# Forming the Strassen sums of w_out: 160 transfers of 256 KB through SBUF tiles, or 16 transfers of 2 MB inside DRAM

## The chip, the core and the metric

The kernel runs on one core of one Trainium2 chip. A core has a matrix engine (TensorE, PE in the profile, with its weight loads as PEld), a vector engine (VectorE, DVE), a scalar engine (ScalarE, ACT), GpSimd (POOL) and SyncE (SP), which here issues transfers only. Sixteen DMA engines move data between DRAM and the on-chip memory SBUF, and also from DRAM to DRAM. Transfers that SP issues appear in the profile as queue q1, those that POOL issues as queue q0. The metric is the device time of one execution in microseconds; lower is better.

## The reference, cut to what matters

The reference computes one layer of a streaming encoder on 512 rows (T) of 2048 features (D), in float32:

```python
h = rmsnorm(x, g_pre[i])
proj = h @ w_in[i]
qkv, z_a, b_raw, a_raw, glu_in, z_b, gate_logits = jnp.split(proj, _split_points(), axis=-1)
...                                   # gated delta rule on qkv -> y_a, conformer convolution on glu_in -> y_b
mixed = (gate_a * y_a + gate_b * y_b) @ w_out[i]
x = x + rmsnorm(mixed, g_post[i])
e = p[i] @ w_ple_proj[i]
x = x + rmsnorm(jax.nn.sigmoid(x @ w_ple_gate[i]) * e, g_ple[i])
```

The change touches the product with `w_out` (2048 x 2048) alone. The kernel computes it by Strassen's scheme on 2 x 2 blocks of the weight, which needs four sums of blocks: T1 = B11 + B12, T3 = B12 + B22, T2 = T1 + B22 and T4 = T2 + B21. (The signs are in the operands on the other side.) Each block, in each of two column halves `jp`, is four pieces of 512 KB: 2 MB.

## The kernel before, in words

Every large product is done on the PE with float32 split in two parts, high and low, so that a product of one weight tile and one activation tile is three matmuls of 128 x 128 by 128 x 512. A weight piece comes from DRAM into a raw tile (SP issues it), ACT casts the high part (line 127 or 408), DVE or POOL forms the low part by a subtraction (line 128 or 308), and the PE reads both.

The stages, with the times at which the trace of before shows their matmuls:

- 0 to 45 us, `load_x` (lines 226 to 266). SP issues, in this order, pieces of `w_ple_proj` and of `x`, one row block of x (two transfers of 512 KB) for each piece; then constants, the first piece of `w_in`, sixteen stores of 256 KB to `pe_dram` (line 257), and then the next three pieces of `w_in`. For each row block ACT squares x (line 245), DVE forms a mean, POOL takes it to the power -1/2 (`xrs`, line 250), and DVE scales x (line 252). Meanwhile the PE multiplies `p` by `w_ple_proj` (lines 216 to 218). Then it transposes x (line 261) and begins on the z_b part of `w_in` (lines 184, 186, 188).
- 45 to 95 us, the first five tiles of z_b, in the same loop `gemm_cm`.
- 95 to 551 us, `z_phase`: three weight groups (z, ga, gb), each with two column halves, by the same Strassen scheme (matmuls on lines 421 to 423). Here the weight sums are formed as they are used: raw pieces in tiles `raw` and `zraw`, sums on DVE in `zt`, and the last block added by an accumulating transfer from POOL (line 369, 48 of them). Up to eight finished weight pieces stand ready for the PE in the pools `ring` and `zw` (four each).
- 551 to 1480 us, q, k, v and the delta rule head by head, with further parts of `w_in`, in `gemm_cm`. Side jobs are spread among the matmuls by `tick()`: each job is a generator that is advanced once in so many matmuls.
- 1480 to 2086 us, convolution, the branch products (`yp`).
- 2088 to 2249 us, the product with `w_out` (`f`, lines 1385 to 1387), which loads the sums from the DRAM tensor `wo_sums`.
- 2249 to 2436 us, the per-layer embedding.

`presum` (line 1002) forms the sums of `w_out` ahead of time. It is spawned as a side job after the first pair of heads (line 1040). In before it does it piece by piece: it takes blocks into SBUF tiles `wsum` out of the pool `slots` (21 tiles shared by all), some by accumulating transfers, and gives sums to `wo_sums`.

The order in which each engine's instructions stand is not that of the Python text. A scheduler places the whole program's instructions on each engine when the program is built. It keeps the dependencies, gives tiles out as they come free, and puts an instruction on an engine when its own reckoning says that it can go. So an instruction whose inputs are ready and which needs no tile can stand far ahead of its place in the text. On the chip each engine then takes its instructions strictly in that order, POOL and its transfers too.

Of the kernel before, what the change touches and what calls it, by code (L numbers as in the profile page):

```python
# [9 lines left out]
F32 = mybir.dt.float32  # L10
F32R = mybir.dt.float32r
AF = mybir.ActivationFunctionType
ALU = mybir.AluOpType
AX = mybir.AxisListType.X

P = 128
T = 512
# [64 lines left out]
def _body(ctx, tc, A, out):  # L82
    nc = tc.nc
# [7 lines left out]
    slots = ctx.enter_context(tc.tile_pool(name="slots", bufs=21, side="right"))  # L91
# [47 lines left out]
    jobs = deque()  # L139
    active = []  # L140

    def spawn(gen, period, key=None):
        active.append([gen, period, period, key])
# [24 lines left out]
    def w_in_tile(t):  # L168
        return A["w_in"][t]

    def gemm_cm(src, rhs, evac):
        if src is not None:
            prep_src.extend([src[0], src[1]])

        def job():
            ps = gps.tile([P, T], F32, tag="g", name="g")
            for qt in range(4):
                hi, lo = next_piece()
                for kk in range(4):
                    k = qt * 4 + kk  # L180
                    rh, rl = rhs[k]
                    wh = hi[:, kk * P:(kk + 1) * P]
                    wl = lo[:, kk * P:(kk + 1) * P]
                    mm(ps, wh, rh, start=(k == 0), stop=False)  # L184
                    tick()
                    mm(ps, wh, rl, start=False, stop=False)  # L186
                    tick()
                    mm(ps, wl, rh, start=False, stop=(k == NK - 1))  # L188
                    tick()
            evac(ps)  # L190
        jobs.append(job)
# [99 lines left out]
    B11, B12, B22, B21 = range(4)  # L291
# [369 lines left out]
    def evac_k(h):  # L661
        def f(ps):
            y = conv4(ps, 16 + h)
            kc = hd.tile([P, T], F32, tag="kc", name="kc", bufs=2)
            nc.scalar.activation(kc, y, AF.Silu)
            kq = hd.tile([P, NTT, 4, 64], F32, tag="kq", name="kq", bufs=4)
            nc.gpsimd.tensor_copy(kq[:, :, 0::3, :], kc.rearrange("p (t x i) -> p t x i", x=2, i=64))
            hstate[h].update(kc=kc, kq=kq)
        return f

    def evac_q(h):
        def f(ps):
            y = conv4(ps, h)
            nc.scalar.activation(hstate[h]["kq"][:, :, 1:3, :], y.rearrange("p (t x i) -> p t x i", x=2, i=64), AF.Silu)
        return f

    def evac_v(h):
        def f(ps):
            y = conv4(ps, 32 + h)
            vc = hd.tile([P, T], F32, tag="vc", name="vc", bufs=2)  # L680
            nc.scalar.activation(vc, y, AF.Silu)
            hstate[h].update(vc=vc)
        return f
# [315 lines left out]
    WO = A["w_out"]  # L999
    T1, T2, T3, T4 = range(4)  # L1000
    sums = dram.tile([2, 4, 4, P, 1024], F32, name="wo_sums")
    def presum():
        for jp in range(2):
            for q in range(4):
                cs = [slice(n * T, n * T + T) for n in range(2)]
                a = [slots.tile([P, T], F32, tag="s", name="wsum") for n in range(2)]

                def take(t, blk, add):
                    for n in range(2):
                        nc.gpsimd.dma_start(t[n], WO[jp, blk, q][:, cs[n]], **(dict(accum_op=ALU.add) if add else {}))  # L1010
                        yield

                def give(t, m):
                    for n in range(2):
                        nc.gpsimd.dma_start(sums[jp, m, q][:, cs[n]], t[n])
                        yield
                yield from take(a, B11, False)
                b = [slots.tile([P, T], F32, tag="s", name="wsum") for n in range(2)]
                yield from take(b, B12, False)
                yield from take(a, B12, True)  # L1020
                yield from take(b, B22, True)
                yield from give(a, T1)
                yield from give(b, T3)
                yield from take(a, B22, True)
                yield 24
                yield from give(a, T2)
                yield from take(a, B21, True)
                yield 24
                yield from give(a, T4)

    rest = deque([lambda i=i: zb_tile(i) for i in range(FILL, NK)] + [f for i in range(2) for f in (lambda i=i: glu_b(i), lambda i=i: glu_a(i))])
    for g in range(NH // 2):
        pair = (2 * g, 2 * g + 1)
        for h in pair:
            gemm_cm(w_in_tile(16 + h), hT, evac_k(h))
            gemm_cm(w_in_tile(h), hT, evac_q(h))
            gemm_cm(w_in_tile(32 + h), hT, evac_v(h))
        jobs.append(lambda g=g: spawn(group(g), HP, "heads"))
        if g == 0:
            jobs.append(lambda: spawn(presum(), 13, "presum"))  # L1040
        for _ in range(2):
            if rest:
                rest.popleft()()
# [584 lines left out]
    for tt in range(NTT):  # L1628
# [9 lines left out]
        for j in range(4):  # L1638
            s = e_t4[tt][j]
# [67 lines left out]
```

## Time and profile before

| | |
|---|---|
| median of 3 runs | 2436.77 us (2436.03 to 2437.53) |
| the profiled execution | 2438.2 us, its span 2436.4 us |
| PE busy | 2409.8 us of the span (99%) |
| DVE, ACT, POOL busy | 1785.5, 1208.0, 491.8 us |
| moved by DMA | 380.21 MB, mean 156 GB/s; by SP's queue 319.32 MB, by POOL's 54.54 MB |
| `presum`'s transfers | 96 into `wsum` and 64 out of it, 256 KB each, issued from 552.6 to 1219.4 us |

In the rows of a timeline the first number is the start in microseconds from the span's start, the second how long the group took; in brackets stands how long the engine was idle before, and what ended that. A row of windows gives, for a stretch of time, its length, the busy time of PE, PEld, DVE, ACT and POOL (with the count of instructions), the granted clock of the PE, the mean busy share of the 16 DMA engines, and what they moved in GB/s. A row of waits gives who waited for whom: the total, how often, the longest.

### The profile page before, as it was taken

The numbers are of one execution on the slowest core, as the hardware profiler recorded it, in microseconds if no ns is written. First come the engines' busy times: TensorE is split into PE (matmuls) and PEld (weight loads), VectorE is DVE, ScalarE is ACT, GpSimd is POOL, SyncE is SP. The second block draws the span as 40 slices with busy tenths as digits, with TensorE's granted clock in tenths as the row PEclk, the third lists the DMA queues.
The fourth block names the chain that finished last, engine by engine and source line by source line (L and its number), as shares of the span: only waits on it lengthen the run. The fifth ranks groups of instructions, "written<-read, shape, count | busy, mean of one in ns | idle before, by whom it ended". The sixth has DMA issues, their size and how long they took to land.

```text
span 2436.4 us, 33721 instructions
## 1 busy us (share of the span) xinstructions
PE 2409.8 (99%) x11962; PEld 1983.6 (81%) x11962; DVE 1785.5 (73%) x3355; ACT 1208.0 (50%) x2357; POOL 491.8 (20%) x521
## 2 busy tenths in 40 slices
PE   8999999999999999999999999999999999999998
PEld 7888888887788888888888887888887788788886
DVE  7878888777677776767777668999998654667644
ACT  6555545555655555554556554454424433554532
POOL 0001110013213031232200002998840000000000
PEclk9999999999999999999999999999999999999999
DMA  7567776757546262556522222443534332664552
GB/s 264 168 194 208 195 207 206 212 155 210 175 122 182 94 181 92 169 166 184 173 92 92 77 87 74 151 135 110 168 125 164 126 124 97 234 218 168 194 175 77
DMA packets 145289, 380.21 MB, mean 156 GB/s; under 512 B 16352, under 2 KB 24800, under 8 KB 145120
## 3 DMA queue, kind: packets, MB, share of 16 engines
q1 hardware_dynamic: 119008, 319.32, 39.3%
q0 software_dynamic: 23808, 54.54, 10.3%
q10 hardware_dynamic: 2304, 4.20, 0.5%
q8 instruction: 94, 1.54, 0.3%
q14 instruction: 75, 0.61, 0.1%
HBM read 329.75 MB, written 48.23 MB: 155 GB/s over the span
## 4 chain that ended last, share of the span: by engine, by line
PE 94%; DVE 3%; ACT 1%; issue 1%; DMA 1%; POOL 0%; SPq 0%; DVEq 0%; POOLq 0%; ACTq 0%
PE g L186 14%; PE g L188 14%; PE g L184 14%; PE zp L422 6%; PE zp L421 6%; PE zp L423 6%; PE yp L1095 4%; PE yp L1097 4%; PE yp L1093 4%; PE f L1385 2%; PE f L1386 2%; PE f L1387 2%; PE f L1558 2%; PE f L1557 2%; PE f L1556 2%; PE psB L709 1%
## 5 line engine op out<-in xcount | busy, mean ns | idle before, releaser
L186 PE MATMUL g<-hl,w 128*128 128x512 f32 x1536 | 610.4, 397 | 0.0
L188 PE MATMUL g<-hh,w 128*128 128x512 f32 x1536 | 609.2, 397 | 0.0
L184 PE MATMUL g<-hh,w 128*128 128x512 f32 x1536 | 608.3, 396 | 0.1
L127 ACT CAST w<-raw 128x512 fp32r<-128x512 f32 x588 | 357.6, 618 | 454.7 <-PE g L188 176.7
L128 DVE TENSOR_TENSOR w<-raw,w 128x512 fp32r<-128x512 f32 x474 | 327.2, 697 | 180.3 <-ACT w L127 177.4
L188 PEld LDWEIGHTS g<-hh,w 128*128 128x128 f32 x1536 | 289.0, 188 | 56.3 <-DVE w L128 2.6
L186 PEld LDWEIGHTS g<-hl,w 128*128 128x128 f32 x1536 | 289.0, 188 | 55.7 <-issue 1.4
L184 PEld LDWEIGHTS g<-hh,w 128*128 128x128 f32 x1536 | 289.1, 188 | 54.2 <-ACT w L127 0.5
L955 DVE SCALAR_TENSOR_TENSOR uc<-up,vec,uc 128x497 f32<-128x497 f32 (+29 forms) x390 | 282.3, 734 | 13.2 <-ACT uc L934 1.9
L128 POOL TENSOR_TENSOR w<-raw,w 128x512 fp32r<-128x512 f32 x114 | 146.6, 1301 | 59.6 <-ACT w L127 57.8
L656 DVE SCALAR_TENSOR_TENSOR cv<-g,vec,cv 128x511 f32<-128x511 f32 x144 | 106.4, 739 | 27.6 <-ACT cv L654 26.9
L1093 PE MATMUL yp<-w,uh 128*128 128x512 f32 x256 | 100.1, 393 | 0.9 <-DVE gt L1104 0.9
L1095 PE MATMUL yp<-w,uh 128*128 128x512 f32 x256 | 100.3, 392 | 0.1
L1095 PE MATMUL yp<-w,oh 128*128 128x512 f32 x256 | 100.1, 391 | 0.0
L1097 PE MATMUL yp<-w,ul 128*128 128x512 f32 x256 | 100.1, 392 | 0.0
L1097 PE MATMUL yp<-w,ol 128*128 128x512 f32 x256 | 99.5, 391 | 0.0
L1093 PE MATMUL yp<-w,oh 128*128 128x512 f32 x256 | 99.1, 389 | 0.0
L842 DVE TENSOR_TENSOR prod<-UT,VT 128x2 f32<-128x2 f32 (+30 forms) x248 | 87.5, 353 | 6.5
L1010 POOL DMA_DIRECT2D wsum<-in_w_out x96 | 75.4, 840 | 67.7 <-DMA wsum<-in_w_out 35.5
L1329 POOL TENSOR_TENSOR rmsm<-totm,mhalf_c 128x2 f32<-128x2 f32 x2 | 2.4, 1202 | 377.3 <-DVE totm L1327 377.3
L977 POOL TENSOR_TENSOR uc<-uc,pr 128x511 f32<-128x511 f32 (+29 forms) x60 | 76.0, 1267 | 8.3 <-ACT pr L976 7.7
L1385 PE MATMUL f<-wsp,oph 128*128 128x512 f32 x192 | 75.6, 393 | 1.7 <-ACT wsp L1366 1.7
(386 smaller groups left out, 4943.4 us busy)
## 6 DMA issues: line engine op xcount, KB each, us to landing
raw<-in_w_in SPq DMA_DIRECT2D x194, 512.0 KB, 3.4
wsum<-in_w_out POOLq DMA_DIRECT2D x96, 256.0 KB, 5.2
raw<-in_w_ple_gate SPq DMA_DIRECT2D x40, 512.0 KB, 3.9
wo_sums<-wsum POOLq DMA_DIRECT2D x64, 256.0 KB, 4.1
raw<-in_w_br_a SPq DMA_DIRECT2D x32, 512.0 KB, 3.3
raw<-in_w_br_b SPq DMA_DIRECT2D x32, 512.0 KB, 3.3
raw<-in_w_ga SPq DMA_DIRECT2D x24, 512.0 KB, 4.4
raw<-in_w_gb SPq DMA_DIRECT2D x24, 512.0 KB, 4.7
```

Source lines behind the costliest of these rows:

```text
L127: nc.scalar.copy(hi, rq)
L128: low_part[0].tensor_tensor(lo, rq, hi.bitcast(F32), ALU.subtract)
L184: mm(ps, wh, rh, start=(k == 0), stop=False)
L186: mm(ps, wh, rl, start=False, stop=False)
L188: mm(ps, wl, rh, start=False, stop=(k == NK - 1))
L421: mm(ps[pr][t], lh, wh, start=q + n == 0, stop=False)
L422: mm(ps[pr][t], ll, wh, start=False, stop=False)
L423: mm(ps[pr][t], lh, wl, start=False, stop=q == 3 and n == 1)
L955: pin(nc.vector.scalar_tensor_tensor(y[:, s:], u[:, 0:T - s], vv(w0 + TAPS - 1 - s), y[:, s:], ALU.mult, ALU.add))
L1093: mm(ps[tt], lh[:, b], wh, start=k == 0, stop=False)
L1095: mm(ps[tt], lh[:, b], wl, start=False, stop=False)
L1097: mm(ps[tt], ll[:, b], wh, start=False, stop=k == NK - 1)
```

## The change

Instead of 512 KB pieces that go through SBUF, `presum` moves whole blocks of 2 MB from DRAM to DRAM, in eight transfers for each column half: T1 = B11 and T3 = B12 as plain copies of `w_out`'s blocks, B12 and B22 added to them by accumulating transfers, T2 as a plain copy of T1 out of `wo_sums` and B22 added, T4 as a plain copy of T2 and B21 added. The plain ones go out as 32 rows of 16384 numbers (64 KB), the accumulating ones as 256 rows of 2048 numbers (8 KB). No tile of `slots` is used. The job's period is 130 matmuls in place of 13. What is computed and what is read later is as before. The change makes the file five lines shorter, so that lines after it have numbers five lower.

```diff
     def presum():
         for jp in range(2):
-            for q in range(4):
-                cs = [slice(n * T, n * T + T) for n in range(2)]
-                a = [slots.tile([P, T], F32, tag="s", name="wsum") for n in range(2)]
-
-                def take(t, blk, add):
-                    for n in range(2):
-                        nc.gpsimd.dma_start(t[n], WO[jp, blk, q][:, cs[n]], **(dict(accum_op=ALU.add) if add else {}))
-                        yield
-
-                def give(t, m):
-                    for n in range(2):
-                        nc.gpsimd.dma_start(sums[jp, m, q][:, cs[n]], t[n])
-                        yield
-                yield from take(a, B11, False)
-                b = [slots.tile([P, T], F32, tag="s", name="wsum") for n in range(2)]
-                yield from take(b, B12, False)
-                yield from take(a, B12, True)
-                yield from take(b, B22, True)
-                yield from give(a, T1)
-                yield from give(b, T3)
-                yield from take(a, B22, True)
-                yield 24
-                yield from give(a, T2)
-                yield from take(a, B21, True)
-                yield 24
-                yield from give(a, T4)
+            def put(m, blk, add):
+                nc.gpsimd.dma_start(sums[jp, m], WO[jp, blk], **(dict(accum_op=ALU.add, max_dma_last_dim=8192) if add else {}))
+
+            def copy(m, n):
+                nc.gpsimd.dma_start(sums[jp, m], sums[jp, n])
+            put(T1, B11, False)
+            yield
+            put(T3, B12, False)
+            yield
+            put(T1, B12, True)
+            yield
+            put(T3, B22, True)
+            yield
+            copy(T2, T1)
+            yield
+            put(T2, B22, True)
+            yield
+            copy(T4, T2)
+            yield
+            put(T4, B21, True)
+            yield
...
         if g == 0:
-            jobs.append(lambda: spawn(presum(), 13, "presum"))
+            jobs.append(lambda: spawn(presum(), 130, "presum"))
```

Since the new transfers need no tile, the scheduler places them elsewhere than the old ones. The first place is the beginning of POOL's instructions. `xrs` is the power of the mean for one row block of x, `zt` an accumulating transfer of the z phase, `Tc` to `vz` are cleared just after the z phase. Before:

```order
L100 MEMSET half_c 128x8
L102 MEMSET mhalf_c 128x8
L250 ISA
L250 TENSOR_TENSOR xrs<-xms,mhalf_c 128x1 x4
L369 DMA zt<-in_w_z 128x512 x16
L369 DMA zt<-in_w_ga 128x512 x16
L369 DMA zt<-in_w_gb 128x512 x16
L529 MEMSET Tc 128x512
```

Now, as far as the last group of the z phase begins:

```order
L102 MEMSET mhalf_c 128x8
L1005 DMA wo_sums<-in_w_out 32x16384
L250 ISA
L250 TENSOR_TENSOR xrs<-xms,mhalf_c 128x1 x2
L1005 DMA wo_sums<-in_w_out 32x16384
L250 TENSOR_TENSOR xrs<-xms,mhalf_c 128x1 x2
L1005 DMA wo_sums<-in_w_out 256x2048
L369 DMA zt<-in_w_z 128x512 x8
L1005 DMA wo_sums<-in_w_out 256x2048
L369 DMA zt<-in_w_z 128x512 x8
L1008 DMA wo_sums<-wo_sums 32x16384
L369 DMA zt<-in_w_ga 128x512 x8
```

The copy of T1 now stands ahead of everything of x, that of T3 between the second and the third row block, and the first accumulating transfer (T1 += B12) right behind the fourth; the following ones stand one behind each eight `zt` transfers of the z phase.

The second place is POOL behind the z phase, where before the first of the 160 transfers stood:

```order
L536 MEMSET Xz_4994 128x128
L537 MEMSET vz_4998 128x128
L828 COPY VT<-cst 128x256
L1010 DMA wsum<-in_w_out 128x512 x6
L1015 DMA wo_sums<-wsum 128x512 x3
```

and now the second column half begins:

```order
L536 MEMSET Xz_4994 128x128
L537 MEMSET vz_4998 128x128
L1005 DMA wo_sums<-in_w_out 32x16384
L667 COPY kq<-kc 128x4x2x64
L628 TENSOR_TENSOR tg<-cst,gl 128x512 x2
```

So the first half (`jp` = 0) has moved ahead of and into the z phase, and the second half stands where the first began. SP's own transfers stand in the same order as before through load_x and the first tiles of z_b.

## The prediction

> **What bounds the kernel now.** I read the page's busy times first, then the chain, then the PE's waits.
>
> ```profile
> PE 2409.8 (99%) x11962; PEld 1983.6 (81%) x11962; DVE 1785.5 (73%) x3355; ACT 1208.0 (50%) x2357; POOL 491.8 (20%) x521
> PE 94%; DVE 3%; ACT 1%; issue 1%; DMA 1%; POOL 0%; SPq 0%; DVEq 0%; POOLq 0%; ACTq 0%
> PE e_ps L216 <- ACT w L127: 6.1, 1, 6.1
> ```
>
> The PE is busy for 2409.8 of 2436.4 us and makes 94% of the chain; its idle time is 26.6 us in all, of which 6.1 us are the wait for the very first weights. So almost nothing can be won by freeing POOL, SBUF tiles or DMA engines. What can be lost is large: anything that makes the PE wait adds to the end one for one. The question is whether the moved transfers make it wait.
>
> Next I looked at how full the DMA engines are, by stretches: the first 60 us, the z phase, and the two stretches over which the old presum ran (552.6 to 1219.4 us).
>
> ```profile
> 0.00:10.00 10.00, 3.89 (x9) 2.77 (x10) 1.99 (x3) 3.77 (x5) 0.35 (x6) 1.00 0.80 265
> 10.00:20.00 10.00, 7.81 (x33) 5.83 (x32) 6.08 (x13) 7.41 (x15) 1.11 (x2) 1.00 1.02 402
> 20.00:30.00 10.00, 10.00 (x46) 8.19 (x45) 7.54 (x16) 8.37 (x16) 1.10 (x2) 1.00 1.04 404
> 30.00:40.00 10.00, 10.00 (x71) 8.81 (x70) 9.46 (x15) 7.61 (x14) 0.00 (x0) 1.00 0.90 320
> 40.00:50.00 10.00, 10.00 (x51) 8.18 (x50) 10.00 (x18) 5.72 (x11) 0.00 (x0) 1.00 0.23 80
> 80.00:530.00 450.00, 450.00 (x1987) 372.62 (x1986) 363.16 (x585) 229.92 (x386) 42.87 (x48) 1.00 0.69 198
> 552.00:680.00 128.00, 126.41 (x593) 101.09 (x592) 90.25 (x198) 70.23 (x124) 41.46 (x53) 1.00 0.67 196
> 680.00:1230.00 550.00, 549.94 (x3259) 453.95 (x3259) 393.50 (x982) 302.73 (x712) 122.81 (x169) 1.00 0.52 150
> ```
>
> Three things are to be seen. From 10 to nearly 40 us all 16 DMA engines are full, at 402 GB/s: this is the one stage where a transfer more delays every transfer behind it. In the z phase they are 69% busy while the PE never idles (450.00 of 450). And where the old presum ran, the PE lost 1.6 us (128.00 less 126.41) and nothing after 680 us.
>
> **What is removed.** 160 transfers and their tiles between 552 and 1220 us. POOL waited for them, the PE did not. All that can come back is the 1.6 us of the row 552:680, and part of that belongs to other waits; I take -1, with bounds 0 and -1.6.
>
> **The price of a 2 MB transfer.** No row shows one from DRAM to DRAM; the nearest are these:
>
> ```profile
> q1 hardware_dynamic: 119008, 319.32, 39.3%
> q0 software_dynamic: 23808, 54.54, 10.3%
> zt<-in_w_z POOLq DMA_DIRECT2D x16, 256.0 KB, 5.7
> wsum<-in_w_out POOLq DMA_DIRECT2D x96, 256.0 KB, 5.2
> wo_sums<-wsum POOLq DMA_DIRECT2D x64, 256.0 KB, 4.1
> ```
>
> Queue q1 has plain transfers only: 39.3% of 2436.4 us over 319.32 MB is 3.0 us of all engines for a MB, 6.3 us for 2.1 MB; at the 402 GB/s of the full stretch it is 5.2 us. Queue q0 took 10.3%, 250.9 us, for 54.54 MB. Of these, 32 takes and 64 gives of 0.262 MB are plain (25.2 MB, 75.5 us at q1's price). The rest, 175 us, is 48 zt and 64 accumulating takes, 29.4 MB: 6.0 us a MB, 12.5 us for 2 MB, twice a plain one.
>
> A copy inside DRAM reads and writes DRAM. If both pass at once it costs what one side costs, 5.2 us; if one after the other, a load and a store, 10.4. I take the middle, 8. The accumulating one reads two operands and writes one: two passes are 10.4, three are 15.7, and the row of those into SBUF gives 12.5. I take 13, close to that row.
>
> The Trainium skill ("DMA: Bandwidth & Descriptors", section "Latency and other measured facts") gives copies between DRAM tensors at full rate as 207 to 214 GB/s for each direction. By it a 2 MB copy is an estimated 9.8 us, and the sum below would be 3.6 us higher. No run shows it yet.
>
> **The start.** The order puts T1's copy right behind a memset on POOL, the copy of T3 behind the second `xrs`, T1's accumulation behind the fourth. When these stood, and what SP has under way:
>
> ```profile
> 0.77 0.10 POOL L102 MEMSET mhalf_c<- 128x8 f32 x1
> 18.43 0.56 POOL L250 TENSOR_TENSOR xrs<-xms,mhalf_c 128x1 f32<-128x1 f32 x1 [5.60 <-DVE xms L248]
> 29.26 0.55 POOL L250 TENSOR_TENSOR xrs<-xms,mhalf_c 128x1 f32<-128x1 f32 x1 [4.94 <-DVE xms L248]
> 2.58 7.92 DMA x<-in_x
> 10.59 1.16 ACT xjunk L245 x2
> 12.30 0.50 PE L216 MATMUL e_ps<-w,ph 128*128 128x512 f32 x1 [1.18 <-ACT ph L203]
> 18.93 15.56 SPq L257 DMA_DIRECT2D pe_dram<-e_sb  x16
> 34.54 1.54 SPq L122 DMA_DIRECT2D raw<-in_w_in  x3
> DMA to landing us min/median/max: 5.4/6.7/7.3
> 42.70 1.77 ACT L127 CAST w<-raw 128x512 fp32r<-128x512 f32 x3
> 45.73 0.39 PE L184 MATMUL g<-hh,w 128*128 128x512 f32 x1
> ```
>
> (The landing row is that of line 122 in the stretch 34 to 36.2 us, the three transfers above it.)
>
> *T1 = B11* begins at about 1 us, as SP's first loads do. The chain of waits goes through the x load (2.58 to 10.50), ACT's squares behind it and the cast of `ph`, for which the PE waits until 12.30. There is no slack here, since ACT begins 0.1 us after the landing. So what the copy takes from the engines is added to that landing: +8 (5.2 to 10.4).
>
> *T3 = B12 and T1 += B12* then fall into the full stretch. They stand on another queue than SP's, but SP's queue is never empty here (sixteen stores, then w_in), so once they are done it is late by their whole time, however the two queues share. Who is hurt? The PE begins with w_in's first piece, loaded before. The 25th matmul on it, at 45.73, needs the second piece, issued at 34.54, landed 5.4 us later, at 39.9. A cast (0.6 us) must lie between, so it may land as late as about 45: a slack of 5 us. The fourth `xrs` moves with the rest, so the accumulation still falls ahead of that landing. Price: 8 + 13 - 5 = +16 (5.2 + 10.4 - 5 = 10.6, to 10.4 + 15.7 - 5 = 21.1).
>
> POOL itself holds nothing up. An issue of 256 KB took it 0.9 us or less, no `xrs` stands behind a wait for T1's landing, and the `zt` transfers come 70 us later.
>
> *After a wait.* The first matmuls after the 6.1 us wait come slowly:
>
> ```profile
> 7.86 0.63 PE L216 MATMUL e_ps<-w,ph 128*128 128x512 f32 x1
> 8.29 0.63 PE L217 MATMUL e_ps<-w,ph 128*128 128x512 f32 x1
> 15.07 0.39 PE L216 MATMUL e_ps<-w,ph 128*128 128x512 f32 x1
> 15.30 0.39 PE L217 MATMUL e_ps<-w,ph 128*128 128x512 f32 x1
> ```
>
> They stand 0.43 us apart, later 0.23. From 6.11 to 9.99 there were nine, so the slow start cost 1.8 us. The two waits that I forecast are as long or longer; whether they bring the slow start back no row shows: 0 to 3.6 us, I take +2. The Trainium skill ("TensorE: Matmul & The Clock Gate", section "Part 1: The HAM clock gate") says that an idle window of some 3.4 us takes the array back to half rate; by it the term would be the full 3.6.
>
> **The z phase.** Behind each eight `zt` transfers, at some 76 us from each other, comes one: three accumulations (T3, T2, T4) and two copies, 3 x 13 + 2 x 8 = 55 us of all engines in 450.
>
> ```profile
> L369 POOL DMA_DIRECT2D zt<-in_w_z x16: 866/894/1222, 113.6 to 213.8; - x16
> ACT w L408 <- PE zp L423: 59.8, 74, 3.5
> ACT zw L408 <- PE zp L423: 47.3, 68, 0.8
> DVE zt L308 <- DMA raw<-in_w_z: 9.1, 4, 4.0
> ACT w L408 <- DMA zraw<-in_w_z: 3.3, 2, 2.7
> ```
>
> ACT mostly waits for the PE to give a piece's buffer back (59.8 and 47.3 us): the weights are ahead. Eight pieces may stand ready, each good for six matmuls of 0.226 us (450 us over 1987), 10.9 us when all are full. But some loads are taken as they land (9.1 us and 3.3 us of waits for them), so the lead is not always there. A 13 us accumulation delays the loads beside it by at most 13, of which the lead takes most; an 8 us copy hides. Bounds: 0, and 3 x (13 - 8) = 15 where the lead stands at 8. I take +4. If the cover is gone altogether it is the 55 us.
>
> **The second half** falls on 530 to 900 us, where SP's loads alone left half of the engines free and the old presum's 160 transfers cost no more than the 1.6 us above: 0.
>
> **The sum**, on the profiled execution's 2438.2 us: +8 + 16 + 2 + 4 - 1 = +29, 2467. The median of the runs stands 1.4 us lower, so 2466. Own range of this case: 2436.8 + 5.2 + 10.6 + 0 + 0 - 1.6 = 2451 to 2436.8 + 10.4 + 21.1 + 3.6 + 15 = 2487.
>
> **The rivals.**
>
> 1. *SP's loads keep their pace* (not slower). If the engines take so little of POOL's queue while SP's is full that the x loads and the second w_in piece come no later than their slack, the new transfers trickle through the gaps behind 40 us (share 0.23 in the row 40:50) and nothing is lost; with 1.6 us of the row 552:680 back it is 2435. It decides at one point: x's first block landing by 10.6 us and w_in's second piece by 45. For it: POOL's transfers land within 4.1 to 5.7 us beside SP's, so neither queue is starved. That speaks against it as well, since a fair share is what hurts. Chance 0.10.
> 2. *Only the first copy is felt.* If T1's copy costs its 8 us, but then the fourth `xrs` and T1's accumulation come so late that w_in's second piece lands ahead of it, T3's copy alone is left, within 3 us of the slack: 8 + 3 - 1 = +10, 2447. For it: x and the PE are pushed back by T1 as SP's queue is, but POOL's order is tied to x's last row block. Against it: SP's queue is late by the same. Chance 0.17.
> 3. *The z phase loses its lead.* If the 55 us there are not hidden, since loads that are taken as they land have none, the loss is 55 in place of 4: 2466 + 51 = 2517; half of it 2491. Against it: 107 us of ACT's waits for the PE. Chance 0.13.
>
> The forecast has the other 0.60. "Faster" and "slower" count beyond 0.2%, 4.9 us, about what a measurement of this kernel can tell from no change. Rival 1 alone can be faster or the same: faster 0.02, same 0.09, slower 0.89. The range takes in the forecast, rival 2 and the lower part of rival 3, and leaves out rival 1: 2443 to 2490.
>
> **What would show it.** Right: the first wait of the PE for `ph` or `w` in the first 15 us grows by about 8 us; matmuls of line 186 or 184 wait for a cast of line 127 behind `raw<-in_w_in` for about 10 to 20 us near 60 us; in the windows the DMA share is full until about 70 us; in the z phase waits of the PE for pieces of a few us behind each accumulation; nothing new behind 560 us. Wrong: the z_b matmuls begin at 38 us as before (rival 1); the second w_in piece lands ahead of the first accumulation (rival 2); PE idle time of over 15 us between 95 and 551 us (rival 3). Landings of the 2 MB transfers far from 8 and 13 us on idle engines would show the prices wrong; a copy of 20 us at the start would put the time over 2480.

## The result, and the profile after

The changed kernel takes 2746.45 us (median of five runs, 2740.77 to 2749.87) against 2437.36 us (five runs, 2436.03 to 2439.5): the ratio is 1.1267, 95% interval 1.1254 to 1.128. It is slower, as forecast, but by 309 us where 29 were forecast.

The page of the changed kernel, span and busy times:

```profile
span 2742.8 us, 33547 instructions
PE 2501.5 (91%) x11962; PEld 2044.2 (75%) x11962; DVE 1793.4 (65%) x3355; ACT 1210.1 (44%) x2355; POOL 390.6 (14%) x377
```

The PE does the same 11962 matmuls, but is idle for 241.3 us (2742.8 less 2501.5) where it was idle for 26.6, and its matmuls take 91.7 us longer in all (2501.5 less 2409.8). So the loss of 306 us in the profiled executions has two parts: waits, 215 us more than before, and slow matmuls, 92 us.

Where? The groups of zp (z phase) and py (heads) give the first and the last start of their matmuls. Before:

```profile
L421 PE MATMUL zp<-w,hh x144: 389/389/389, 94.8 to 549.7; 128*128 128x512 f32 x144
L423 PE MATMUL zp<-w,hh x144: 389/389/389, 95.3 to 550.2; 128*128 128x512 f32 x144
L863 PE MATMUL py<-Tc,W x256: 191/191/212, 690.3 to 1444.4; 32*32 32x32 f32 x128
```

After:

```profile
L421 PE MATMUL zp<-w,hh x144: 389/389/628, 117.1 to 612.3; 128*128 128x512 f32 x144
L423 PE MATMUL zp<-w,hh x144: 387/389/794, 117.6 to 612.7; 128*128 128x512 f32 x144
L863 PE MATMUL py<-Tc,W x256: 191/218/258, 889.3 to 1750.8; 32*32 32x32 f32 x128
```

From these I cut the span in four: up to the first zp, from there to the last zp, from there to the last py (called "heads" below), and the rest. The same cuts serve for every run of this study:

| us | start | z phase | heads | rest |
|---|---|---|---|---|
| before | 94.8 | 455.4 | 894.2 | 992.0 |
| after | 117.1 | 495.6 | 1138.1 | 991.9 |
| difference | +22.3 | +40.2 | +243.9 | 0.0 |

Four fifths of the loss lie in the heads, where the forecast had nothing. The longest waits of the PE there (614 to 1755 us):

```profile
PE py L863 <- DVE Tc L857: 102.6, 7, 31.8
PE r_ps L633 <- DVE E_mk L638: 26.5, 5, 13.2
```

And windows of the same kernel, two in the first part of the heads, one in the last:

```profile
720.00:960.00 240.00, 160.46 (x758) 126.53 (x757) 107.08 (x242) 85.32 (x199) 23.36 (x25) 0.79 0.36 103
1200.00:1250.00 50.00, 19.03 (x140) 15.20 (x140) 28.76 (x90) 15.35 (x33) 0.40 (x1) 0.50 0.00 0
1360.00:1760.00 400.00, 400.00 (x2371) 330.42 (x2371) 284.71 (x717) 223.32 (x518) 26.39 (x33) 1.00 0.27 89
```

The kernel before, over all of its heads, for comparison:

```profile
552.00:1445.00 893.00, 891.35 (x5124) 733.00 (x5124) 635.98 (x1561) 492.81 (x1116) 177.12 (x238) 1.00 0.48 140
```

In the row from 1200 to 1250 us the DMA engines are idle (0.00) and the PE still works for only 19.03 of 50 us, at a granted clock of 0.50. No transfer is in the way there. The timeline of the PE in that stretch shows what is:

```profile
1194.76 0.82 PE L807 MATMUL pg<-kq 128*64 128x128 f32 x11
1195.64 0.36 PE L814 MATMUL pe<-sq,cst 128*128 128x8 f32 x2
1227.78 0.28 PE L863 MATMUL py<-Tc,W 32*32 32x32 f32 x2 [31.78 <-DVE Tc L857]
```

Between `pe` and `py` of a pair of heads DVE works through a chain of 31 small steps (`prod` and `VT`, lines 842 and 843) that ends in `Tc` (line 857). Before, the PE did big matmuls of `gemm_cm` meanwhile. Now it has none to do. The order of the PE's instructions tells why. The number of big matmuls (lines 184, 186, 188) that stand between `pe` and the first `py`, for the eight pairs of heads:

| | between pe and py |
|---|---|
| before | 184 in each |
| after | 0, 0, 0, 156, 184, 184, 184, 184 |

In the first three pairs 113, 364 and 364 big matmuls stand in one run right ahead of `pg` instead. Since an engine takes its instructions strictly in order, they can't fill the wait any more. So the first theory, A: the time is lost through the order of the instructions, which the scheduler changed when it was given the new transfers. The rival, B: the 2 MB transfers themselves hold up the loads and stores of the heads stage.

### The profile page after: what moved, and what is told of

It reads as the page before. It is cut to its first block, busy times and chain, and to the rows that moved or that the text cites. A ratio compares the mean times of both kernels' runs of the same rounds, so it can differ in the third digit from the quotient of the medians.

```text
span 2742.8 us, 33547 instructions
## 1 busy us (share of the span) xinstructions
PE 2501.5 (91%) x11962; PEld 2044.2 (75%) x11962; DVE 1793.4 (65%) x3355; ACT 1210.1 (44%) x2355; POOL 390.6 (14%) x377
## 4 chain that ended last, share of the span: by engine, by line
PE 66%; DVE 6%; ACT 2%; issue 2%; DMA 1%; POOL 0%; DVEq 0%; POOLq 0%; ACTq 0%; SPq 0%
PE g L186 12%; PE g L188 12%; PE g L184 12%; PE yp L1090 4%; PE yp L1092 4%; PE yp L1088 4%; PE f L1380 2%; PE f L1381 2%; PE f L1382 2%; PE f L1553 2%; PE f L1552 2%; PE f L1551 2%; DVE prod L842 2%; PE psB L709 1%; PE psS L715 1%
## 5 line engine op out<-in xcount | busy, mean ns | idle before, releaser
L863 PE MATMUL py<-Tc,W 32*32 32x32 f32 x256 | 8.1, 215 | 102.6 <-DVE Tc L857 102.6
L863 PEld LDWEIGHTS py<-Tc,W 32*32 32x32 f32 x256 | 6.7, 128 | 105.4 <-issue 102.3
L423 PE MATMUL zp<-w,hh 128*128 128x512 f32 x144 | 58.9, 409 | 28.6 <-DVE w L308 28.6
## 6 DMA issues: line engine op xcount, KB each, us to landing
wo_sums<-in_w_out POOLq DMA_DIRECT2D x8, 2048.0 KB, 15.3
```

## The experiments

**The PE in the order of the text.** The changed kernel with the big matmuls pinned to the order of the program text (184 between `pe` and `py` again); the transfers are left to the scheduler, as in the changed kernel.

```diff
-                    mm(ps, wh, rh, start=(k == 0), stop=False)
+                    pin(mm(ps, wh, rh, start=(k == 0), stop=False))
...
-                    mm(ps, wh, rl, start=False, stop=False)
+                    pin(mm(ps, wh, rl, start=False, stop=False))
...
-                    mm(ps, wl, rh, start=False, stop=(k == NK - 1))
+                    pin(mm(ps, wl, rh, start=False, stop=(k == NK - 1)))
```

> The transfers stay where the changed kernel has them, but the PE's big matmuls (lines 184, 186, 188) are pinned to the order of the program text, in which 184 of them stand between pe and py of each pair of heads, as in the kernel before. Theory A (the order of the PE's instructions in the heads stage costs the time, since the PE waits for DVE's chain with nothing put in between): the 245 us of the heads stage go, the start and the z phase keep their loss of about 60 us: 2480 to 2520 us. Theory B (the 2 MB transfers themselves hold up the loads and stores of the heads stage): the transfers are as before, so at least 2650 us.

Measured: 2555.85 us, ratio 1.0489 (1.0475 to 1.0504). Start 119.4, z phase 497.0, heads 940.2, rest 997.4 us. 198 of the 244 us in the heads are gone, the start and the z phase keep their loss. It is more than the 2520 expected by A, and far from B's 2650. The rest needed a control, the same three pins in the kernel before:

> The kernel before with the big matmuls (lines 184, 186, 188) pinned to the order of the text, and nothing else changed: the control for the first run, which had 98.35 us of PE work in each 100 us of the heads where the kernel before has 100.00. If that loss belongs to the pinning, this kernel loses it too: 1.65% of the 890 us of the heads, 2445 to 2460 us. If it belongs to the 2 MB transfers, 2437 us.

Measured: 2468.26 us, ratio 1.0126 (1.0109 to 1.0143), heads 918.4 us, rest 997.8 us. The pins cost 24.2 us in the heads and 5.8 behind them, 31 in all, a little over what I expected. So what is left of the changed kernel's loss in the heads, with this order, is 940.2 less 918.4, 21.8 us. One part of it can be read from the waits for `E_mk`, a tile with one buffer that a store to `e_dram` must give back. With the 2 MB transfers (600 to 1560 us), and then the control without (552 to 1470 us):

```profile
PE r_ps L633 <- DVE E_mk L638: 15.6, 3, 12.7
```

```profile
PE r_ps L633 <- DVE E_mk L638: 2.6, 2, 2.2
```

13 of the 22 us are this wait. The store behind the longest of them was issued at 674.5 us and landed at 685.0, as the accumulation of 671.8 did (685.6). So B is true, but small; where the other 9 us come from was not sought.

**The transfers held at their place, and the same transfers written otherwise.** If the order is what counts, a kernel with the same transfers and another order must tell. `pin` ties each transfer to its place in the text (none ahead of 550 us). Then the same with source and destination written as 512 rows of 1024 numbers in place of 4 x 128 x 1024. The transfers in the program are the same in both, 32 x 16384 and 256 x 2048 numbers. (The diff is that of the second kernel; the first has the pins alone.)

```diff
+            rows = lambda t: t.rearrange("q p c -> (q p) c")
...
-                nc.gpsimd.dma_start(sums[jp, m], WO[jp, blk], **(...))
+                pin(nc.gpsimd.dma_start(rows(sums[jp, m]), rows(WO[jp, blk]), **(...)))
...
-                nc.gpsimd.dma_start(sums[jp, m], sums[jp, n])
+                pin(nc.gpsimd.dma_start(rows(sums[jp, m]), rows(sums[jp, n])))
```

> All sixteen 2 MB transfers are tied to their place in the text, so that none goes out ahead of 560 us. The order of the PE's instructions now has none or few big matmuls between pe and py in seven of eight pairs of heads, where the changed kernel has it in four. Both theories: the start and the z phase come back (551 us at the end of the z phase as before). Theory A (order): the loss in the heads is about 245 us for four pairs, so 400 to 500 us for seven or eight: 2830 to 2940 us. Theory B (transfers): sixteen in place of eight there, also about twice 245 us. This run separates them only beside the next one.

> As the run with the transfers held at their place in the text, but source and destination are written as 512 rows of 1024 numbers in place of 4 x 128 x 1024: the same transfers, the same packets, nearly the same places on POOL. The scheduler now leaves 184 big matmuls between pe and py in each pair of heads, as before. Theory A (order): no loss, 2430 to 2445 us, and at most 1.6 us faster than before. Theory B (transfers): as the run before this one, some 2700 us or more.

Measured: held as 4 x 128 x 1024 2876.55 us, ratio 1.1808 (1.179 to 1.1826); held as 512 rows 2438.68 us, ratio 1.0008 (0.9999 to 1.0016). Busy time and the longest waits of the PE, the first and then the second:

```profile
PE 2563.9 (89%) x11962; PEld 2087.0 (73%) x11962; DVE 1802.3 (63%) x3355; ACT 1217.1 (42%) x2355; POOL 389.5 (14%) x377
PE py L863 <- DVE Tc L857: 197.1, 14, 31.8
```

```profile
PE 2411.9 (99%) x11962; PEld 1985.7 (81%) x11962; DVE 1782.8 (73%) x3355; ACT 1208.0 (50%) x2357; POOL 392.7 (16%) x377
PE e_ps L216 <- ACT w L127: 6.2, 1, 6.2
```

All sixteen 2 MB transfers run in the heads in both, and in the second they cost 1.8 us there (896.0 against 894.2). In the second, the instructions of PE, ACT, DVE and SP stand row for row as in the kernel before; in the first, five pairs have no big matmul between `pe` and `py`, one has 48, two have 129 and 156. B falls as the cause in the heads: same transfers, 438 us apart.

**Between the two writings.** The same once more with 16 rows of 32768 numbers.

```diff
-            rows = lambda t: t.rearrange("q p c -> (q p) c")
+            rows = lambda t: t.rearrange("q (a b) c -> (q a) (b c)", b=32)
```

> As the run with the transfers held at their place and written as 512 rows (2438.7 us), but written as 16 rows of 32768 numbers, between that and the 4 x 128 x 1024 of the held run (2876.6 us). Again the same transfers go out in the same packets. The scheduler now leaves 129 to 157 big matmuls between pe and py of each pair of heads, none or one at a time between py, pz and pd, and up to 200 ahead of pg. Theory A (order): between the two, nearer to the 512 rows, since 150 matmuls of 0.226 us are 34 us of cover for a chain of some 32 to 42 us: 2445 to 2560 us. Theory B (transfers): the same as with 512 rows or as with 4, not between.

Measured: 2624.98 us, ratio 1.0768 (1.075 to 1.0786), heads 1093.6 us. It lies between, as A says, but above my range: I had counted the cover of some 150 matmuls as nearly enough.

```profile
PE 2515.7 (96%) x11962; PEld 2039.3 (77%) x11962; DVE 1783.6 (68%) x3355; ACT 1217.3 (46%) x2361; POOL 391.9 (15%) x377
PE py L863 <- DVE Tc L857: 51.1, 8, 7.7
```

The waits did get short (7.7 us at most). But the PE's busy time is 103.8 us over that of the kernel with 512 rows (2515.7 less 2411.9). Over its heads (552 to 1644 us) the mean granted clock is 0.91, where the kernel before has 1.00; the section on the hardware shows where the clock goes.

**The order alone.** Does the loss need any 2 MB transfer? The control (the kernel before, with the pins), with the pauses of the heads' side job between `pg` and the scan taken out, so that its steps follow each other on the PE:

```diff
-        yield 6
...
-            if owed >= 1:
-                yield int(owed)
-                owed -= int(owed)
+            if owed >= 1:
+                owed -= int(owed)
...
-        yield 22
```

(and eight more pauses between these and the scan.)

> As the control (the kernel before, PE in text order, the old 160 transfers), but the pauses of the heads' side job between pg and the scan are taken out, so that no big matmul stands between pe and py. No 2 MB transfer anywhere. Theory A (the order alone costs the time): the PE waits for DVE's chain, some 32 us for each of eight pairs, and its matmuls are slower after it: 240 to 480 us on top of the control, 2690 to 2930 us. Theory B (the 2 MB transfers are needed for the loss): under 2500 us.

Measured: 2780.68 us, ratio 1.1405 (1.1388 to 1.1422), 312 us over the control.

```profile
PE py L856 <- DVE Tc L851: 256.8, 16, 31.8
```

Eight pairs, 32 us each. With no cover, the old transfers of 256 KB lose the same way. For the heads A stands, with and without the new transfers.

**All sixteen at the very start.** The 512 rows without the pins: the scheduler puts all sixteen among POOL's first instructions. PE, ACT, DVE and SP keep the order of before but for a few rows of the PE and of DVE.

> The changed kernel with source and destination written as 512 rows, not held: the scheduler now puts all sixteen transfers at the very start of POOL, and the PE's order in the heads is that of before. Theory A: nothing is lost behind the z phase; all the loss is the contention of the sixteen transfers (8 copies of 9.5 us and 8 accumulations of 15 us, 196 us of all engines) with the loads of the first 300 us: 2500 to 2640 us, most likely 2560. Theory B: no 2 MB transfer runs in the heads stage either, so the same; the run measures the price of the transfers where they meet other traffic.

Measured: 2533.88 us, ratio 1.0397 (1.0383 to 1.0411): start 189.6 (+94.8), z phase 457.6, heads 892.8 us. All of the loss is at the start, about half of the 196 us that the transfers were estimated to take of the engines.

**The first half alone, in two orders.** This pair settles the start and the z phase. First the first half as in the changed kernel, the second half as in the kernel before (two generators, one with `range(1)`, one with `range(1, 2)`):

> The first half as in the changed kernel (eight 2 MB transfers, written as 4 x 128 x 1024, placed by the scheduler at the start and in the z phase, with SP's loads and stores there in the changed kernel's order), the second half as in the kernel before (80 transfers through SBUF). The PE's order in the heads is that of before. If the loss of the changed kernel falls into two independent parts, this keeps the 62 us up to the end of the z phase and loses nothing behind it: 2490 to 2508 us.

Then the first half with its eight transfers at exactly the changed kernel's places on POOL, but as 512 rows and tied there by `pin`, so that PE, ACT, DVE and SP keep the order of before row for row; the second half held in the heads as 512 rows:

```diff
     nc.gpsimd.memset(mhalf_c, -0.5)
+    half = first_half()              # the eight transfers of jp = 0, one for each next()
+    next(half)
...
                 nc.gpsimd.tensor_tensor(rs, ms, mhalf_c[:, 0:1], ALU.pow)
+                if tt % 2:
+                    next(half)
...
                 nc.gpsimd.dma_start(t[n], WZ[grp][jp, blk, q][:, n * T:(n + 1) * T], accum_op=ALU.add)
+            accs[0] += 1
+            if accs[0] % 4 == 0:
+                next(half, None)
```

> The first half's eight transfers stand on POOL exactly where the changed kernel has them (behind the memset, behind the second and the fourth xrs, and one behind each eight zt), but are written as 512 rows, so that SP's and the PE's instructions keep the order of the kernel before; the second half is held in the heads, where it cost nothing. Theory A (beside their own time, the order of SP's and the PE's instructions makes the loss): some 20 us at the start and some 8 us in the z phase, by the 13 us that eight transfers cost there when placed by hand: 2455 to 2480 us. Theory E (the place of the transfers makes the loss, whatever the order): the 62 us of the run above, 2490 to 2508 us.

Measured: 2502.09 us, ratio 1.0271 (1.0254 to 1.0288), and 2456.38 us, ratio 1.008 (1.0065 to 1.0095).

| us | start | z phase | heads |
|---|---|---|---|
| first half as changed | 116.4 | 494.6 | 893.4 |
| same places, order of before | 112.0 | 457.3 | 893.2 |

The 66 us of the first half are two things. With the order of before the transfers cost 20 us, nearly all at the start. With the order of the changed kernel they cost 46 more by the medians and 42 by the profiled executions, of which 37 in the z phase. There the changed kernel has windows like the first of these, the kernel with the order of before the second, each around the same accumulation (T3 += B22), which lands after 16.3 and 16.0 us:

```profile
160.00:200.00 40.00, 32.26 (x137) 26.31 (x136) 23.55 (x37) 15.52 (x27) 1.39 (x2) 0.91 0.76 203
```

```profile
155.00:195.00 40.00, 40.00 (x178) 33.13 (x177) 29.56 (x49) 20.87 (x36) 2.52 (x3) 1.00 0.83 222
```

The longest waits of the PE in the z phase of the changed kernel (117 to 613 us) are these:

```profile
PE zp L423 <- DVE w L308: 28.6, 5, 7.9
```

Four of them are of 5.6 to 7.9 us, and each ends 18 to 20 us after POOL has issued a 2 MB transfer (T3 += B22, the copy of T2, T2 += B22, T4 += B21). So in this stage the order costs time only where it meets a transfer. Rows of ACT, DVE and the PE show how. After T3 += B22 (issued at 165.06 us) in the changed kernel:

```profile
173.01 0.60 ACT L408 CAST w<-zt 128x512 fp32r<-128x512 f32 x1
174.96 0.69 DVE L308 TENSOR_TENSOR zt<-raw,zraw 128x512 f32<-128x512 f32 x1 [2.52 <-DMA zraw<-in_w_z]
181.27 0.69 DVE L308 TENSOR_TENSOR zt<-raw,zraw 128x512 f32<-128x512 f32 x1 [5.62 <-DMA zraw<-in_w_z]
181.88 0.68 DVE L308 TENSOR_TENSOR w<-zt,w 128x512 fp32r<-128x512 f32 x1
182.62 0.79 PE L423 MATMUL zp<-w,hh 128*128 128x512 f32 x1 [7.74 <-DVE w L308]
```

In the kernel with the same places and the order of before (issued at 160.69 us):

```profile
174.34 0.69 DVE L328 TENSOR_TENSOR w<-zt,w 128x512 fp32r<-128x512 f32 x1
176.72 0.69 DVE L328 TENSOR_TENSOR zt<-raw,zraw 128x512 f32<-128x512 f32 x1 [1.09 <-DMA zraw<-in_w_z]
```

On DVE, `zt` from `raw` and `zraw` adds two loaded pieces, and must wait for a load that lands with the 2 MB transfer (181.18 us, the transfer 181.33). `w` from `zt` forms the low part of a piece that the PE reads next. In the changed kernel two such additions stand ahead of the low parts of eight pieces, the first of which ACT had cast at 173.01 us. DVE takes its instructions in order, so those pieces wait for a load that they do not need, and the PE stands still for 7.74 us, until 182.62. With the order of before the low parts come first. The PE's own order in the z phase is that of before in both kernels. SP's differs too, but the time that its stores take does not tell the two apart: eight of them hold SP for 10.8 us here (171.0 to 181.8) and for 10.4 us in the kernel that loses nothing (166.9 to 177.3). No run moved DVE's instructions alone, so this is read from the trace and not tried.

**The z phase: size, or place?** The start of before, the first half's eight transfers one behind each six `zt` transfers, then the same cut into 32 of 512 KB, one or two behind each two `zt`; order of PE, ACT, DVE and SP as before in both. The edit is the last hunk above with 3 in place of 4, and a loop over row ranges of a quarter.

> The first half's eight transfers of 2 MB, written as 512 rows, are put into the z phase, one behind each six zt transfers; the second half stands in the heads, where it cost nothing. The start is that of the kernel before. By the earlier runs four copies of about 8.5 and four accumulations of about 14.5 us are 92 us of all engines. Theory C (the lead of the weights, 8 to 11 us, is what decides: a transfer that holds the loads up for longer costs the rest): 4 x 0 to 3 for the copies and 4 x 4 to 8 for the accumulations: 2455 to 2480 us. Theory D (the engines' time is lost whole since loads taken as they land have no lead): 2500 to 2530 us.

> As the run before this one, with each transfer cut into four of 512 KB, one or two behind each two zt transfers: the same bytes and the same stage, 92 us of the engines, in portions of about 2.1 and 3.7 us. Theory C (lead): each portion is less than the lead, so nothing or little is lost: 2437 to 2450 us. Theory D (engines' time): the same loss as with whole transfers.

Measured: whole 2450.54 us, ratio 1.0053 (1.0038 to 1.0068), z phase 470.6; cut 2452.05 us, ratio 1.0061 (1.0045 to 1.0077), z phase 475.1 us. Neither theory holds. By D the 92 us of the engines would have cost 62 or more; they cost 13 and 14 by the medians (15 and 20 in the z phase of the profiled executions). By C the whole ones would have cost 17 or more and cutting would have saved most of it; they cost less and it saved nothing. And the five transfers of the kernel above cost 2 us in this stage. So where a transfer stands among the loads may count more than its size; that was not tried further.

**What makes an accumulation dear.** As the held kernel with 512 rows, with the copies of T1 and T2 in packets of 8 KB (first half) and 4 KB (second) in place of 64 KB:

> All sixteen transfers held in the heads as 512 rows, where each copy with 64 KB packets took 8.4 to 9 us and each accumulation with 8 KB packets 14 to 16 us. Here the two copies of T1 and T2 out of the sums go out in packets of 8 KB in the first half and of 4 KB in the second. If it is the packets that make an accumulation dear, a copy in 8 KB packets takes 12 us or more; if it is the adding, it stays at 8 to 10 us. The time stays at 2438 us.

Measured: 2439.2 us in one run. Landing times of the four copies in packets of 64 KB (held kernel), and then of the two in 8 KB and of the two in 4 KB:

```profile
DMA to landing us min/median/max: 8.4/8.5/9.1
```

```profile
DMA to landing us min/median/max: 9.7/9.8/10.0
...
DMA to landing us min/median/max: 9.6/10.3/11.0
```

In 8 KB packets a copy takes 1.3 us more, an accumulation (13 to 16 us on engines with little else to do) 4.5 to 7.5 more. So most of it is not the packets' size, as far as two copies of each kind can tell.

## Why the prediction was wrong

*Direction:* right. *Size:* wrong by 280 us, because of one step.

**The step that failed** is "The second half ... 0". Its reason, that the engines have room there, is true: sixteen transfers held in the heads cost 1.8 us. But the step took it for granted that the PE's instructions stand as before, and did not look. The orders that it went by were those of POOL, and of SP through the first z_b tiles; those of the PE in the heads and of DVE at the start and in the z phase had not been compared. The runs put in its place: some 2 us for the transfers if the order stays, +244 with the order that the scheduler made, of which 198 went when the PE alone was given the text's order.

**The z phase, +4** (0 to 15): with the order of before it is +1.9, as forecast; in the changed kernel +40.2, outside the bounds, and most of what lies between comes with the order (37 us in the pair of runs). The term took the pieces that stand ready to cover a late load; by DVE's rows, pieces that were cast and nearly ready could not be used, since they stood behind the late load in DVE's order. Rival 3 had the size (between half and all of 55 us) and the loads that are taken as they land, but not the reason: with the order of before the same loads came as late, and nothing was lost.

**The start, +8 + 16 + 2.** The first wait for `w` grew from 6.1 to 12.7 us: +6.6 for 8. With the order of before (the kernel with the same places) the wait for w_in's second piece is there, and smaller than forecast, 9.6 for 16:

```profile
PE e_ps L234 <- ACT w L145: 12.7, 1, 12.7
PE g L202 <- ACT w L145: 9.6, 1, 9.6
```

The start is 17.2 us longer, so 1.0 is left for the slow matmuls (2). In the changed kernel the second wait is at another place, since the order has changed here too. The PE's wait, and the two rows of DVE around its end (50.56 us):

```profile
PE xp L261 <- issue: 12.9, 1, 12.9
48.50 1.29 DVE L128 TENSOR_TENSOR w<-raw,w 128x512 fp32r<-128x512 f32 x2 [10.12 <-ACT w L127]
49.71 2.73 DVE L252 TENSOR_SCALAR x<-x,xrs 128x1024 f32<-128x1024 f32 x4
```

DVE waits for the cast of w_in's second piece (landed at 47.8 us), and the scaling of x for the PE's transposes stands behind it, though its `xrs` were there by 23.3 us. So the late load was the one forecast, but the PE met it through DVE's order and by way of x.

Rival 2 had the accumulation of T1 come too late for w_in's second piece, and in the changed kernel it did (53.9 us against a landing at 47.8), without the gain that rival 2 drew from it; with the order of before it was issued at 34.3, as forecast.

**The prices, 8 and 13 us.** On engines with little else to do 8.4 to 9.1, and 13 to 16; in the full stretch a copy took 10.3 us (23.27 to 33.59). These are near the upper ends of the bounds. Beside the loads of the z phase the copies took 11.1 and 14.1 us and the accumulations 15.3 to 17.1, mostly above those bounds. The Trainium skill ("DMA: Bandwidth & Descriptors", section "Latency and other measured facts") gave an estimate of 9.8 us. The trace is faster, and decides: 2.097 MB in 8.4 us are 250 GB/s from issue to landing, where that page has 207 to 214.

**The removal, -1:** with the order of before nothing came back (ratio 1.0008).

So the sum would have been nearly right for the kernel with the order of before: 2456.4 us with the first half at the same places, 20 us over its kernel before where 29 were forecast. No version of the change that was run gains: held where the engines have room, and with the order of before, it takes as long as the kernel before, since what it removes was hidden.

What stays open is why the scheduler reckons so. The three writings differ in the outermost dimension alone, 4, 16 and 512 rows, with the same transfers in the program, and the fewer rows, the worse the order: 2877, 2625 and 2439 us. That it takes a transfer for the slower the fewer its outermost rows are fits all of these. It is argued, not shown: no run shows the scheduler's own times.

## What to carry to other kernels

Where a scheduler places the instructions, a change in one job can move the work of every engine. Compare the order on the engine that sets the end, and on those that feed it, over the whole program, before costing anything: count what stands between a step and the one that waits for its result, and look for an instruction that waits for a load ahead of others that are ready. And when transfers get a new shape, write them with many rows in the outermost dimension and tie them to a place where the DMA engines have room; here the same bytes then cost 2 us (2438.68 against 2437.11, not to be told from 0) in place of 309.

## What the runs showed of the hardware

**The PE's clock comes down in a wait, and stays down through small matmuls.** The changed kernel, the pair of heads of the timeline above:

```profile
1196.00:1204.00 8.00, 0.00 (x1) 0.00 (x0) 0.62 (x4) 7.68 (x4) 0.00 (x0) 0.71 0.10 35
1204.00:1212.00 8.00, 0.00 (x0) 0.00 (x0) 6.87 (x32) 0.00 (x0) 0.00 (x0) 0.50 0.00 0
1244.00:1252.00 8.00, 7.81 (x27) 6.01 (x27) 4.28 (x13) 3.71 (x12) 0.00 (x0) 0.50 0.00 1
1268.00:1276.00 8.00, 7.40 (x28) 5.96 (x29) 4.71 (x16) 3.04 (x17) 2.42 (x4) 0.60 0.41 133
1276.00:1284.00 8.00, 7.95 (x65) 6.07 (x64) 3.66 (x8) 5.11 (x20) 0.90 (x2) 1.00 0.00 0
```

In the first 8 us without work the mean clock is 0.71, in the next 0.50; a full clock for 3.4 us and then half of it gives this 0.71. At 1228 the PE works again, busy 7.8 of 8 us from 1244 on, and the clock stays at 0.50 through 1268. The mean of 0.60 in the row from there is 1.6 us of full clock, so it came back at about 1274, after 46 us. Until 1270 this is the scan, matmuls of 128 columns in steps that depend on each other; the big matmuls begin at 1270.6. So a wait costs its own length and then the slow stretch behind it: of the 306 us, 92 are slower matmuls. I had allowed 2 us. The Trainium skill ("TensorE: Matmul & The Clock Gate", section "Part 1: The HAM clock gate") has the clock fall after an idle window of some 3.4 us, with which the trace agrees, and rise after as long of sustained work, which a PE shown as 97% busy by the profile did not bring here as long as its matmuls were those of the scan.

**Loads beside a 2 MB accumulation land late.** In the z phase of the kernel before, the `zraw` loads of 256 KB landed 3.1 to 9.7 us after their issue, with a median of 6.0. In the changed kernel those issued beside T3 += B22 (162 to 166 us) took up to 16.7 us, as the accumulation did:

```profile
DMA to landing us min/median/max: 6.6/8.8/16.7
```

With the order of before they took 8.7 to 17.5 us beside the same transfer, no less, and the PE lost nothing (40.00 of 40.00 us in the window shown above).
